# Padding tiles that move three groups of matmul operands to other offsets within a 512-byte line

## The chip, the cores and the metric

The kernel runs on one core of one Trainium2 chip. The metric is the device time of one execution in microseconds (us); the time given for a kernel is the median of its runs.

## The reference

Two layers of a decoder trunk on 512 tokens of width 1024, everything in float32. Each layer is a half-step feed-forward block, a mixer, and a second half-step feed-forward block:

```
def swiglu(h, w_up, w_down):
    gate, up = jnp.split(h @ w_up, 2, axis=-1)
    return (jax.nn.silu(gate) * up) @ w_down
...
for l in range(DEPTH):
    x = x + 0.5 * swiglu(rms_norm(x, ffn1_norm[l]), ffn1_w_up[l], ffn1_w_down[l])
    h = rms_norm(x, mix_norm[l])
    proj = h @ w_in[l]
    q, k, v, z, xbc, dt_raw, gate_sb, gate_ssm = jnp.split(proj, IN_SPLITS, axis=-1)
    ... y_sb = stick_breaking_attention(q, k, v) @ w_branch_sb[l]      # 4 heads x 128
    ... y_ssm = mamba2_mixer(z, xbc, dt_raw, ...) @ w_branch_ssm[l]    # 24 heads x 64, 8 groups
    merged = sigmoid(gate_sb) * y_sb + sigmoid(gate_ssm) * y_ssm
    x = x + merged @ w_out[l]
    x = x + 0.5 * swiglu(rms_norm(x, ffn2_norm[l]), ffn2_w_up[l], ffn2_w_down[l])
return rms_norm(x, final_norm)
```

The hidden width of the feed-forward block is 2816, that is 22 blocks of 128.

## The kernel before

**Layout.** All activations are kept transposed: a tile has 128 channels in its 128 partitions and the 512 tokens along the free axis (2048 bytes of a partition). A weight unit is 128 x 1024 floats: eight blocks of 128 x 128, one per block of input channels.

**Products in three parts.** TensorE works on rounded float32 (`fp32r`). To keep full precision each operand is split into a rounded part and a rest: weights into `whi` and `wlo` (`convert`, L282 on ScalarE and L284 on VectorE), normalised inputs into `hhi` and `hlo`, hidden activations into two `act` tiles, and so on. `mm3` (L315 to L317) then issues three matmuls for each 128 x 128 block: high weights by high input, low weights by high input, high weights by low input. Each of the three loads a stationary operand of 128 x 128 (a load of weights, which runs beside the matmul before it) and streams a moving operand of 256 or 512 columns. In most units the weights are stationary and the activations move; in `by_tokens` (v and z) it is the other way round.

**The feed-forward block** (`ffn`) runs three slices of 8, 8 and 6 hidden blocks. Most hidden blocks are computed in pairs by `pair_of_blocks`, which gets two blocks' gate and up products for both halves of the tokens from seven half-width products (`SEVEN`) on sums of weights and on differences of inputs. The differences are made once per block by `combine`: their rounded parts are the tiles `th`, their rests the tiles `tl`, and the products on them have 256 columns. Four of the seven products (s2, s1, s3 and 22) move `th` and `tl`; the other three (11, 12 and s4) move halves of `hhi` and `hlo`. The activated results are split into `act` tiles, and the `down` units multiply these, 512 columns at a time, into the output.

**The mixer** (`mixer`) makes q, k and v (tiles `yt`), runs the attention, whose outputs are the tiles `ohi` and `olo` of pool `yo`, then the convolution and the state-space scan, whose outputs are again `yt` tiles. The branch products `bsb` (moving `ohi`, `olo`) and `bssm` (moving `yt`) and the output projection `out` (moving `mhi`, `mlo`) follow.

**Order.** The whole program is in an order written by hand: each engine executes its instructions in the order of issue. Side work (activations, splits, conversions of the next weight units) is held in generators, and `tick` advances them by a step after each group of matmuls, so that VectorE, ScalarE and GpSimd work beside TensorE. Weights are fetched by the SP queue four units ahead and converted two units ahead.

**Where tiles lie.** Tile pools are stacked: those of the left side grow from low addresses of a partition, those with `side="right"` grow downwards from the top. Nearly all tiles are multiples of 512 bytes long, so that a pool gives its offset within a 512-byte line to all of its tiles and to the pools stacked on it. In the program before, these offsets are:

| tiles | side | offset in a 512-byte line | less the weights' offset |
|---|---|---|---|
| `whi`, `wlo` (weights), `wraw` | left | 96 | 0 |
| `hhi`, `hlo` | left | 96 | 0 |
| `act`, and stacked on it `s1`, `s2`, `s3`, `g`, `a`, `c` | left | 96 | 0 |
| `mhi`, `mlo`, most tiles of the mixer's pool | left | 96 | 0 |
| `x`, and `uv`, `th`, `tl` stacked on it | right | 480 | 384 |
| `yo` (`ohi`, `olo`), `yt`, under a tile `edge` of 384 bytes | right | 96 | 0 |

The tile `edge` is allocated and never written or read.

Of the kernel before, what the change touches and what calls it, by code (L numbers as in the profile page):

```python
# [17 lines left out]
P = 128  # L18
# [95 lines left out]
def pairs_from(layer, f):  # L114

    return 6 if (layer, f) == (0, 1) else 2


def unit_order(layer):

    def ffn(f):
        for s, (j0, j1) in enumerate(SLICES):
# [7 lines left out]
            for m in OUT_ORDER:  # L130
                yield (layer, f, "down", s, m), j1 - j0

    yield from ffn(1)
    for t, h in qkv_order():
        yield (layer, t, h), KB
# [13 lines left out]
    for m in OUT_ORDER:  # L149
        yield (layer, "out", m), KB  # L150
    yield from ffn(2)


# [10 lines left out]
class Builder:  # L164
# [581 lines left out]
    def ffn(self, layer, f, gain, gain_next):  # L746
        tc = self.tc
        with tc.tile_pool(name=f"act{layer}{f}", bufs=8, reuse_waits="tile") as ap, \
                tc.tile_pool(name=f"sx{layer}{f}", bufs=2, reuse_waits="tile") as self.sx, \
                tc.tile_pool(name=f"ffn{layer}{f}", bufs=3, reuse_waits="tile") as fp:  # L750
            self.gated = {}
            for s, (j0, j1) in enumerate(SLICES):
                act = []
                last = s == len(SLICES) - 1
                for j in range(j0, j1):
                    if j % 2 == 0:
                        two = self.pair(ap, ("act", "act"), (P, 2 * SEQ))
                        act += [tuple(t[:, i * SEQ:(i + 1) * SEQ] for t in two) for i in range(2)]
                    if j >= pairs_from(layer, f):
                        if j % 2 == 0:  # L760
                            self.pair_of_blocks((layer, f, "pair", j), fp, two)
                        continue
                    g = self.t(fp, [P, SEQ], "g", bufs=4)
                    if self.pos == 0:
                        pg, pu = self.opening(gain)
                        self.spawn(self.gate(pg, g))
                        for k in range(KB // 2):
                            self.spawn(self.combine(k, gain), 12 + 14 * k)
                    else:
                        pg = self.product(self.h, layer, f, "gate", j)  # L770
                        self.spawn(self.gate(pg, g))
                        pu = self.product(self.h, layer, f, "up", j)
                    self.spawn(self.up(pu, g, fp, act[-2 + j % 2]))
                n, both = j1 - j0, []
                for m in OUT_ORDER[:2]:
                    both.append((self.t(self.pmm, [P, SEQ], "mm"), self.unit(layer, f, "down", s, m, ahead=m == 0)))
                    self.dense(*both[-1], act, 0, n - 2, stop=False)
                for i, m in enumerate(OUT_ORDER):
                    if last and gain_next is None and i == KB - 3:
                        self.ending((layer, f, "down", s), act, n, fp)  # L780
                        break
                    if i < 2:
                        if i:
                            self.ahead(1)
                        ps = both[i][0]
                        self.dense(*both[i], act, n - 2, n, start=False, base=0)
                    else:
                        ps = self.t(self.pmm, [P, SEQ], "mm")
                        self.dense(ps, self.unit(layer, f, "down", s, m), act, 0, n)
                    if last and i == 0:  # L790
                        self.norm_start()
                        self.xd = self.t(self.dr, [KB, P, SEQ], "xd") if f == 1 else None
                        if f == 1:
                            self.close_t()
                    self.spawn(self.down(ps, m, gain_next, last))
# [476 lines left out]
    def mixer(self, layer):  # L1272
# [13 lines left out]
        with ExitStack() as mix:  # L1286
            enter = mix.enter_context
            branches = ExitStack()
            edge = branches.enter_context(
                tc.tile_pool(name=f"edge{layer}", bufs=1, side="right", reuse_waits="tile"))  # L1290
            self.t(edge, [P, 96], "edge")
            self.yo = branches.enter_context(
                tc.tile_pool(name=f"yo{layer}", bufs=SBH, side="right", reuse_waits="tile"))
            self.yt = branches.enter_context(
# [88 lines left out]

    def open_t(self):

        self.tpool = self.tc.tile_pool(name=self.name("tpool"), bufs=2, side="right", reuse_waits="tile")
        self.tp = self.tpool.__enter__()

    def close_t(self):
        self.tpool.__exit__(None, None, None)  # L1390
        self.tp = None

    def build(self):
# [141 lines left out]
```

## Time and profile before

| | |
|---|---|
| median of 3 runs | 2582.1 us (2581.85 to 2583.41) |
| the profiled execution | 2582.94 us, its span from the first to the last instruction 2581.2 us |
| TensorE matmuls (PE) | 15028, busy 2559.8 us of the span |
| TensorE loads of weights (PEld) | 15028, busy 2288.4 us |
| VectorE (DVE) / ScalarE (ACT) / GpSimd (POOL) | busy 1752.4 / 1282.0 / 498.5 us |
| granted TensorE clock | 0.999 of full speed |

In the trace the rows of successive matmuls overlap, and the ends of matmuls are modelled. A row's duration is therefore longer than the time that a product costs in a dense stretch; that time is the distance from one start to the next, which is called the pitch here.

### The profile page before, as it was taken

What the parts mean: (1) busy time and instruction counts of PE and PEld (TensorE: products, weight loads), DVE (VectorE), ACT (ScalarE), POOL (GpSimd) and SP (SyncE); (2) the same over time, 40 slices, a digit from 0 to 9 for tenths busy, and PEclk for the clock granted to TensorE, in tenths of its full rate; (3) what the DMA queues carried; (4) which work ended last, traced back from release to release, by engine and by line L of the source; (5) the groups of instructions that cost most, each with busy time, mean ns of one, the idle gap of its engine ahead of it and who ended that gap; (6) DMA issues with size and microseconds to landing.
All of it is one profiled execution on the core that took longest, in us unless ns stands there. A gap on an engine that the chain in (4) does not pass through costs nothing.

```text
span 2581.2 us, 38169 instructions
## 1 busy us (share of the span) xinstructions
PE 2559.8 (99%) x15028; PEld 2288.4 (89%) x15028; DVE 1752.4 (68%) x2426; ACT 1282.0 (50%) x2103; POOL 498.5 (19%) x614
## 2 busy tenths in 40 slices
PE   9999999999999999999999999999999999999998
PEld 7898988888888889899998989888888888899997
DVE  8575875676664478586885858756676644876766
ACT  6343556665554255343653535566555533543444
POOL 0121201143341002121121312012333310022120
PEclk9999999999999999999999999999999999999999
DMA  6454542233333454545364545423333334455452
GB/s 183 138 159 136 132 138 87 99 103 110 101 105 107 139 162 139 164 139 164 106 180 139 156 141 136 139 72 111 99 103 104 116 109 143 152 143 168 142 162 78
DMA packets 104659, 335.76 MB, mean 130 GB/s; under 512 B 11872, under 2 KB 15392, under 8 KB 104480
## 3 DMA queue, kind: packets, MB, share of 16 engines
q1 hardware_dynamic: 92672, 292.84, 34.2%
q0 software_dynamic: 10944, 39.85, 8.6%
q8 instruction: 118, 1.93, 0.3%
q10 hardware_dynamic: 864, 0.64, 0.1%
q14 instruction: 61, 0.50, 0.1%
HBM read 320.60 MB, written 12.68 MB: 129 GB/s over the span
## 4 chain that ended last, share of the span: by engine, by line
PE 93%; DVE 4%; ACT 2%; issue 1%; DMA 0%; POOL 0%; SPq 0%; DVEq 0%; ACTq 0%
PE mm L315 26%; PE mm L317 25%; PE mm L316 25%; PE pa L316 3%; PE pa L317 3%; PE pa L315 3%; PE pa L1169 2%; DVE wlo L284 1%; PE pa L1171 1%; PE pt L853 1%; PE pt L1154 1%; DVE cv L1027 1%; PE pt L1152 1%; ACT whi L282 1%; PE pa L453 0%
## 5 line engine op out<-in xcount | busy, mean ns | idle before, releaser
L282 ACT CAST whi<-wraw 128x1024 fp32r<-128x1024 f32 (+3 forms) x440 | 435.1, 989 | 584.9 <-PE mm L317 485.0
L284 DVE TENSOR_TENSOR wlo<-wraw,whi 128x1024 fp32r<-128x1024 f32 (+3 forms) x440 | 538.7, 1224 | 165.9 <-ACT whi L282 164.5
L315 PE MATMUL mm<-hhi,whi 128*128 128x512 f32 (+1 forms) x1584 | 565.1, 357 | 0.0
L317 PE MATMUL mm<-hlo,whi 128*128 128x512 f32 (+1 forms) x1584 | 554.1, 350 | 0.4 <-DVE hlo L507 0.4
L316 PE MATMUL mm<-hhi,wlo 128*128 128x512 f32 (+1 forms) x1584 | 553.0, 349 | 0.0
L317 PEld LDWEIGHTS mm<-hlo,whi 128*128 128x128 f32 x1584 | 299.9, 189 | 40.3 <-DVE hlo L507 0.8
L316 PEld LDWEIGHTS mm<-hhi,wlo 128*128 128x128 f32 x1584 | 300.4, 190 | 34.6 <-DVE wlo L284 0.2
L315 PEld LDWEIGHTS mm<-hhi,whi 128*128 128x128 f32 x1584 | 300.3, 190 | 34.2 <-ACT hhi L505 0.4
L284 DVE TENSOR_TENSOR wlo<-s,whi 128x1024 fp32r<-128x1024 f32 x152 | 235.2, 1561 | 60.4 <-ACT whi L282 60.4
L315 PE MATMUL mm<-act,whi 128*128 128x512 f32 (+1 forms) x710 | 274.2, 386 | 0.0
L317 PE MATMUL mm<-act,whi 128*128 128x512 f32 (+1 forms) x710 | 274.2, 386 | 0.0
L316 PE MATMUL mm<-act,wlo 128*128 128x512 f32 (+1 forms) x710 | 274.1, 386 | 0.0
L315 PE MATMUL mm<-th,whi 128*128 128x256 f32 x912 | 257.4, 282 | 0.0
L317 PE MATMUL mm<-tl,whi 128*128 128x256 f32 x912 | 257.0, 282 | 0.0
L316 PE MATMUL mm<-th,wlo 128*128 128x256 f32 x912 | 256.9, 282 | 0.0
L626 POOL TENSOR_TENSOR g<-g,rs 128x512 f32<-128x512 f32 x76 | 132.5, 1744 | 553.4 <-DVE g L633 534.3
L282 ACT CAST whi<-s 128x1024 fp32r<-128x1024 f32 x152 | 159.3, 1048 | 102.4 <-PE mm L317 60.7
L652 DVE SCALAR_TENSOR_TENSOR x<-mm,x 128x512 f32<-128x512 f32 x93 | 64.1, 689 | 196.0 <-PE mm L317 196.0
L254 POOL DMA_DIRECT2D s<-in_wflat_dram x76 | 65.6, 863 | 621.3 <-DMA s<-in_wflat_dram 332.4
L315 PEld LDWEIGHTS mm<-th,whi 128*128 128x128 f32 x912 | 172.4, 189 | 0.0
L316 PEld LDWEIGHTS mm<-th,wlo 128*128 128x128 f32 x912 | 172.0, 189 | 0.0
L317 PEld LDWEIGHTS mm<-tl,whi 128*128 128x128 f32 x912 | 171.9, 188 | 0.0
(306 smaller groups left out, 5088.9 us busy)
## 6 DMA issues: line engine op xcount, KB each, us to landing
wraw<-in_wflat_dram SPq DMA_DIRECT2D x328, 512.0 KB, 3.6
s<-in_wflat_dram SPq DMA_DIRECT2D x76, 512.0 KB, 4.7
s<-in_wflat_dram POOLq DMA_DIRECT2D x76, 512.0 KB, 7.4
wraw<-in_wflat_dram SPq DMA_DIRECT2D x88, 384.0 KB, 3.1
cumb<-cum_d SPq DMA_DIRECT2D x16, 768.0 KB, 4.8
xd<-x SPq DMA_DIRECT2D x16, 256.0 KB, 3.2
wraw<-in_wflat_dram SPq DMA_DIRECT2D x16, 256.0 KB, 3.6
x<-xd SPq DMA_DIRECT2D x16, 256.0 KB, 3.9
```

The costliest lines, as they stand in the source:

```text
L254: self.nc.gpsimd.dma_start(raw, src, accum_op=ALU.add)
L282: nc.scalar.copy(hi[:, :n], raw[:, :n])
L284: nc.vector.tensor_tensor(lo[:, :n], raw[:, :n], hi[:, :n].bitcast(F32), op=ALU.subtract)
L315: mm(ps, a[0], b[0], start=start, stop=False, **kw)
L316: mm(ps, a[1], b[0], start=False, stop=False, **kw)
L317: mm(ps, a[0], b[1], start=False, stop=stop, **kw)
L626: eng.tensor_tensor(r, r, self.rs[:, cols].unsqueeze(1).to_broadcast([P, 2, half]), op=ALU.mult)
L652: self.nc.vector.scalar_tensor_tensor(x, pd, 0.5, x, op0=ALU.mult, op1=ALU.add)
L853: self.nc.tensor.transpose(pt[:, cs], src[:, cs], self.ident)
L1027: nc.vector.scalar_tensor_tensor(u[:, j:], ps[:, :SEQ - j], tap[KCONV - 1 - j], u[:, j:], op0=ALU.mult, op1=ALU.add)
L1152: nc.tensor.matmul(pc[:, :P], bt[:, span(c)], ct[:, span(c)], start=True, stop=True)
L1169: nc.tensor.matmul(py[:, i * HD:(i + 1) * HD], decs[c][:, i, :], xdts[c][:, i, :], start=True, stop=True)
```

## The change

Three tiles that nothing writes or reads move the tiles stacked behind them:

- A tile `gap` of 192 bytes is the first of pool `act`. The `act` tiles, and the pools `sx` (`s1`, `s2`, `s3`) and `ffn` (`g`, `a`, `c`) stacked on them, move up by 192 bytes: offset 288, 192 off the weights'.
- A tile `rim` of 320 bytes in a pool of its own is opened just before the pool of `uv`, `th` and `tl`, and closed just after it. These move down by 320 bytes: from offset 480 to 160, 64 off the weights'. The `x` tiles stay.
- The tile `edge` shrinks from 384 to 352 bytes. The tiles of `yo` and `yt` move up by 32 bytes: offset 128, 32 off the weights'.

No instruction, order or transfer is written differently.

```
@@ ffn
             self.gated = {}
+            self.t(ap, [P, 48], "gap", bufs=1)
             for s, (j0, j1) in enumerate(SLICES):
@@ mixer
-            self.t(edge, [P, 96], "edge")
+            self.t(edge, [P, 88], "edge")
@@ open_t
+        self.rim = self.tc.tile_pool(name=self.name("rim"), bufs=1, side="right", reuse_waits="tile")
+        self.t(self.rim.__enter__(), [P, 80], "rim")
         self.tpool = self.tc.tile_pool(name=self.name("tpool"), bufs=2, side="right", reuse_waits="tile")
@@ close_t
         self.tpool.__exit__(None, None, None)
+        self.rim.__exit__(None, None, None)
         self.tp = None
```

`reuse_waits="tile"` means that a new tile waits for the last uses of those older tiles whose bytes it overlaps.

More of the change, by code (lines that the diff above doesn't have):

```diff
@@ L751, in ffn @@
             self.gated = {}
+            self.t(ap, [P, 48], "gap", bufs=1)
             for s, (j0, j1) in enumerate(SLICES):
@@ L1290, in mixer @@
                 tc.tile_pool(name=f"edge{layer}", bufs=1, side="right", reuse_waits="tile"))
-            self.t(edge, [P, 96], "edge")
+            self.t(edge, [P, 88], "edge")
             self.yo = branches.enter_context(
@@ L1384, in open_t @@
     def open_t(self):
+        self.rim = self.tc.tile_pool(name=self.name("rim"), bufs=1, side="right", reuse_waits="tile")
+        self.t(self.rim.__enter__(), [P, 80], "rim")
         self.tpool = self.tc.tile_pool(name=self.name("tpool"), bufs=2, side="right", reuse_waits="tile")
@@ L1390, in close_t @@
         self.tpool.__exit__(None, None, None)
+        self.rim.__exit__(None, None, None)
         self.tp = None
```

## The prediction

> **What bounds the kernel now.** I read the page's busy times first, then its chain of work that ended last.
>
> ```profile
> span 2581.2 us, 38169 instructions
> PE 2559.8 (99%) x15028; PEld 2288.4 (89%) x15028; DVE 1752.4 (68%) x2426; ACT 1282.0 (50%) x2103; POOL 498.5 (19%) x614
> ...
> PE 93%; DVE 4%; ACT 2%; issue 1%; DMA 0%; POOL 0%; SPq 0%; DVEq 0%; ACTq 0%
> PE mm L315 26%; PE mm L317 25%; PE mm L316 25%; PE pa L316 3%; PE pa L317 3%; PE pa L315 3%; PE pa L1169 2%; DVE wlo L284 1%; PE pa L1171 1%; PE pt L853 1%; PE pt L1154 1%; DVE cv L1027 1%; PE pt L1152 1%; ACT whi L282 1%; PE pa L453 0%
> ```
>
> TensorE is on 93% of the chain, and the three matmuls of `mm3` (L315 to L317) alone on 85%. The change adds no instruction, so the only price at stake is the pitch of these products: nanoseconds from one start to the next, times a count. Next the groups of instructions, with shapes kept apart, for the counts. I show the L315 rows; L316 and L317 have as many each, so a group's products are three times its row.
>
> ```profile
> L315 PE MATMUL mm<-hhi,whi 128*128 128x512 f32 x976 | 392.9, 403 | 0.0
> L315 PE MATMUL mm<-act,whi 128*128 128x512 f32 x686 | 267.2, 389 | 0.0
> L315 PE MATMUL mm<-th,whi 128*128 128x256 f32 x912 | 257.4, 282 | 0.0
> L315 PE MATMUL mm<-hhi,whi 128*128 128x256 f32 x608 | 172.1, 283 | 0.0
> L315 PE MATMUL pa<-th,whi 128*128 128x256 f32 x304 | 85.5, 281 | 0.0
> L315 PE MATMUL mm<-yt,whi 128*128 128x512 f32 x192 | 74.8, 390 | 0.0
> L315 PE MATMUL mm<-ohi,whi 128*128 128x512 f32 x64 | 25.3, 396 | 0.0
> L315 PE MATMUL mm<-act,whi 128*128 128x256 f32 x24 | 7.0, 291 | 0.0
> L315 PE MATMUL pa<-act,whi 128*128 128x256 f32 x12 | 3.4, 283 | 0.0
> ```
>
> What the change moves: on `th` and `tl`, 3 x (912 + 304) = 3648 products of 256 columns; on `act`, 3 x 686 = 2058 of 512 columns and 3 x 36 = 108 of 256; on `yt` and `ohi`/`olo`, 3 x (192 + 64) = 768 of 512 columns. Together 2826 of 512 and 3756 of 256. It leaves `hhi`/`hlo` (among them 3 x 976 and 3 x 608 here) at offset 0. The durations (282 and 283, 389 and 390) say nothing on the offset, as their ends are modelled. So I went to the starts, in order of time, at the borders of pure stretches.
>
> ```profile
> 92.85 0.40 PE L315 MATMUL mm<-act,whi 128*128 128x512 f32 x1
> 93.09 0.40 PE L316 MATMUL mm<-act,wlo 128*128 128x512 f32 x1
> 93.32 0.40 PE L317 MATMUL mm<-act,whi 128*128 128x512 f32 x1
> 93.56 0.39 PE L315 MATMUL mm<-act,whi 128*128 128x512 f32 x1
> 93.78 0.39 PE L316 MATMUL mm<-act,wlo 128*128 128x512 f32 x1
> ...
> 94.94 0.39 PE L315 MATMUL mm<-act,whi 128*128 128x512 f32 x1
> ...
> 136.42 0.28 PE L315 MATMUL mm<-hhi,whi 128*128 128x256 f32 x1
> ...
> 142.17 0.28 PE L315 MATMUL mm<-th,whi 128*128 128x256 f32 x1
> ...
> 150.72 0.28 PE L315 MATMUL pa<-hhi,whi 128*128 128x256 f32 x1
> ...
> 470.72 0.33 PE L968 MATMUL pa<-short,ntri 128*128 128x128 f32 x2
> 470.89 0.45 PE L315 MATMUL mm<-hhi,whi 128*128 128x512 f32 x1
> ...
> 885.80 0.39 PE L315 MATMUL mm<-yt,whi 128*128 128x512 f32 x1
> ...
> 902.12 0.39 PE L315 MATMUL mm<-mhi,whi 128*128 128x512 f32 x1
> ```
>
> The counts between these starts come from the busy times by stretch (the number after PE's busy time also holds one or two matmuls whose rows reach in from before: 2, 1, 2 and 1 in the first four).
>
> ```profile
> 92.84:136.41 43.57, 43.57 (x194) 36.07 (x193) 18.86 (x21) 9.58 (x10) 1.73 (x2) 1.00 0.55 168
> 136.41:142.16 5.75, 5.75 (x49) 5.74 (x48) 3.02 (x3) 2.58 (x3) 0.00 (x0) 1.00 0.11 46
> 142.16:150.71 8.55, 8.55 (x74) 8.55 (x73) 6.75 (x6) 4.63 (x6) 5.10 (x4) 1.00 0.63 152
> 885.79:902.11 16.32, 16.32 (x73) 13.52 (x72) 8.00 (x10) 4.41 (x5) 0.00 (x0) 1.00 0.48 148
> 140.00:214.00 74.00, 74.00 (x623) 74.00 (x622) 63.92 (x59) 40.15 (x52) 23.97 (x18) 1.00 0.56 150
> ```
>
> The columns are the stretch, its length, then busy time and count of PE, of the weight loads, DVE, ACT and POOL, the granted clock, the DMA share and GB/s. So:
>
> - `act`, 512 columns, offset 0: 43.57 us / 192 = 226.9 ns. `yt`, offset 0: 16.32 / 72 = 226.7 ns.
> - `hhi`, 256 columns, offset 0: 5.75 / 48 = 119.8 ns.
> - `th`, 256 columns, offset 384: 8.55 / 72 = 118.75 ns.
>
> From 256 to 512 columns at offset 0 the pitch grows by 226.7 - 119.8 = 106.9 ns, so a product costs 106.9 ns for each 256 columns and a fixed 12.9 ns. The fixed part is what an offset can touch. Two readings say that it does. At offset 384 it is 118.75 - 106.9 = 11.85 ns, 1.05 less than at offset 0, in products alike in all but the tiles. And within one stretch at one offset it isn't steady at first: the starts from 92.85 to 94.94 are 0.24, 0.23, 0.24 and 0.22 us apart and nine of them take 2.09 us, 232 ns each, before the stretch falls to 226.7. So the cost depends on how the two reading streams, the moving operand and the next weights, meet, and that has several outcomes.
>
> **The change part by part.** The sum is made against the profiled execution, 2582.94 us (its span is 2581.2), 0.8 above the median of 2582.1.
>
> `rim` (`th`, `tl`): from 384 to 64 off the weights, 3648 products. Upper bound of a gain: two 128-column products from 470.72 to 470.89 take 0.17 us where they stream 2 x 53 ns (half of 106.9 each); the first had its weights loaded beside the matmul before, so the second waited for its own, about 0.17 - 0.06 = 0.11 us. A 256-column product cannot go below its weight load, so 118.75 can fall to some 112: at most 6.7 x 3648 = 24.6 us. On the other side the nearest row is offset 0, 119.8: +1.05 x 3648 = +3.8 us; twice that rise would be +7.7.
>
> `gap` and `edge` (`act`, `yt`, `ohi`, `olo`): from 0 to 192 and 32 off the weights, 2826 products of 512 columns. Upper bound of a gain: all of the fixed 12.9 ns, 36.5 us. On the other side: the 232 ns of the first nine `act` products for good, +5.2 x 2826 = +14.7 us.
>
> Between these ends I take the value near the one offset that the trace compares, which gave 1.05 ns of 12.9, but not at it: that one is an arbitrary offset, and the stretch above swings by 10 ns between neighbours. I take twice it, 2.1 to 2.2 ns, for all three groups: 2.2 x 6582 = 14.5 us. The 108 `act` products of 256 columns are in that count.
>
> The rest has one answer, nothing. The padding issues nothing. VectorE, ScalarE and GpSimd read and write the moved tiles in the same lengths; beside the products in the feed-forward pairs DVE is busy 63.92 of 74.00 us, and that is the cover of a faster TensorE: it would give out only where the pitch falls by more than 14%, and the bound above for `th` is 6%. The stretch with `act` has DVE at 18.86 of 43.57. The new borders let an `act` tile of 4096 bytes reach 192 bytes into one more older tile; the tiles concerned (gates, merged inputs) are read by products that stand ahead on TensorE of those whose results fill `act`, so the wait is over when it is asked for. `th` and `tl` overlap the same two older tiles each, by other amounts. What is queued behind such a wait on ACT (the split's cast) and DVE (its rest) would be the next weight conversions, which are two units ahead, and those units take 24 x 0.119 = 2.9 us each at the least.
>
> Sum: 2582.9 - 14.5 = 2568.4, against the median 2567.6. I predict 2568 us.
>
> A rule stands against the whole change. The Trainium skill (TensorE: Matmul & The Clock Gate, step-by-step part of "What happens when you issue a matmul") says that TensorE has two independent SBUF read ports, one for the moving operand and one for the loads of weights, so that "Loading the next tile's weights doesn't steal SBUF read bandwidth from the running matmul"; SBUF — State Buffer, "Who interferes with whom", adds that "PE and ACT never wait on anyone". By that the offset is worth nothing and the time stays 2582. The pitches of 119.8 and 118.75 do not agree with it for products alike in form, but by 1 ns only; the fixed 12.9 ns may still be something that no offset moves.
>
> **The rivals.**
>
> Nothing changes (0.25). The fixed cost belongs to changing the weights, and the 1.05 ns is a peculiarity of 256 columns, where the load of about 112 ns fills nearly the whole pitch. For it: `act` and `yt` settle on the same 226.7 to 226.9. Against it: the slow start of each `act` stretch. Then only `th` and `tl` move, by -1 to +1 ns: 2582 - 4 to 2582 + 4, that is 2578 to 2586, centre 2582. It is also the case in which the padding doesn't do what it says. The skill's rule above comes to this result.
>
> Most of the fixed cost goes (0.15). At the new offsets the two streams never meet: 12.9 x 2826 + 6.7 x 3648 = 61 us, 2521; I count from a gain of 30 us, 2552, on.
>
> Slower (0.20). One mechanism: at offset 0 the 512-column products settle into an even pitch after nine of them, and at 192 and 32 they never settle. The place is the `down`, `bsb` and `bssm` units, the price 5.2 ns on 2826 products, +14.7 us: 2597. With `th` back at the cost of offset 0 it would be 2601. It decides from 5.2 us / 2826 = 1.8 ns per product on. For it: at 512 columns the even pitch is seen only at offset 0, and the trace has no other offset there. Against it: with 256 columns the mean at 384 is lower, not higher.
>
> **How the numbers follow.** My forecast, a gain of 6 to 30 us (2552 to 2576), has 0.40, the large gain 0.15, no change 0.25, slower 0.20. A measurement of this kernel can tell about 0.2%, 5.2 us. Faster by over 0.2%: 0.40 + 0.15 = 0.55; within: 0.25; slower: 0.20. The time is that of the likeliest case, 2568. For the range I leave out the lower half of the large gain (below 2537, 0.08 to 0.09) and the slower case beyond its own price (above 2598, 0.1): 2537 to 2598. The forecast's own range is 2552 to 2576.
>
> **What would show it.** In the changed kernel's rows of starts, stretches of 72 `th` products should take 116.5 ns each (8.39 us instead of 8.55), the 192 `act` products 224.7 ns (43.1 us instead of 43.57), the 72 `yt` products 224.5 (16.16 us instead of 16.32), while 48 `hhi` products stay at 5.75 us. If `act` and `yt` stay at 226.7 the offset has no hold on 512 columns; if `act` stays near 232 the slower rival has come. If the pitches fall and the span does not, DVE has taken over in the pairs: its idle time there would be gone. What would make the prediction most wrong is that the fixed cost is a threshold thing, all or nothing at an offset: then the gain is several times mine, or the loss is.

## The result: slower by 0.6%, all of it in the products of 512 columns

| | before | after |
|---|---|---|
| median | 2582.2 us | 2597.3 us |
| ratio, 95% interval | | 1.0058 (1.0047 to 1.0070) |
| span of the profiled execution | 2581.2 us | 2595.6 us |

The forecast was 2568 us. The time landed 15.1 us above the kernel before, at the price that the prediction had given its rival "slower" (2597 us).

The page of the changed kernel, first its busy times:

```profile
span 2595.6 us, 38169 instructions
PE 2575.1 (99%) x15028; PEld 2285.6 (88%) x15028; DVE 1754.6 (68%) x2426; ACT 1281.7 (49%) x2103; POOL 500.1 (19%) x614
```

The counts of instructions are the same on each engine; PE is busy 15.3 us longer, no other engine differs by more than 3 us, and the part of the span in which PE is not busy goes from 21.4 to 20.5 us. So there is no new wait: the products themselves take longer. The stretches that answer to those shown before (length, busy time and count of PE, loads of weights, DVE, ACT, POOL, granted clock, DMA share, GB/s):

```profile
137.03:142.78 5.75, 5.75 (x49) 5.73 (x48) 3.02 (x3) 2.59 (x3) 0.00 (x0) 1.00 0.11 43
142.78:151.27 8.49, 8.49 (x74) 8.49 (x73) 6.75 (x6) 4.64 (x6) 5.14 (x4) 1.00 0.59 150
216.86:261.65 44.79, 44.79 (x194) 36.11 (x193) 18.88 (x21) 9.56 (x10) 1.74 (x2) 1.00 0.55 164
890.19:906.99 16.80, 16.80 (x73) 13.50 (x72) 7.93 (x10) 4.40 (x5) 0.00 (x0) 1.00 0.47 141
```

They hold 48 `hhi`, 72 `th`/`tl`, 192 `act` and 72 `yt` products (and one or two rows that reach in). The pitch is 5.75 / 48 = 119.8 ns for `hhi` as before, 8.49 / 72 = 117.9 for `th` (118.75 before), 44.79 / 192 = 233.3 for `act` (226.9) and 16.80 / 72 = 233.3 for `yt` (226.7). With the pitch of one stretch taken for all products of its kind, and that of `yt` for `ohi` and `olo` too:

| moved | pitch | products | us |
|---|---|---|---|
| `th`, `tl` | -0.9 ns | 3648 | -3.3 |
| `act`, 512 columns | +6.4 ns | 2058 | +13.2 |
| `yt`, `ohi`, `olo` | +6.6 ns | 768 | +5.1 |
| sum | | | +15.0 |

That is nearly the whole of the 15.1 us between the medians; the two profiled spans lie 14.4 us apart. The starts show that the slow `act` stretch is not unsteady:

```profile
216.87 0.39 PE L315 MATMUL mm<-act,whi 128*128 128x512 f32 x1
217.09 0.40 PE L316 MATMUL mm<-act,wlo 128*128 128x512 f32 x1
217.33 0.40 PE L317 MATMUL mm<-act,whi 128*128 128x512 f32 x1
...
218.26 0.40 PE L315 MATMUL mm<-act,whi 128*128 128x512 f32 x1
...
261.66 0.28 PE L315 MATMUL mm<-hhi,whi 128*128 128x256 f32 x1
```

The second product starts at 217.09 and the seventh at 218.26: five pitches of 0.234 us, the same as in the whole stretch. It has settled at once, in another and dearer cycle. The groups of instructions show the same:

```profile
L315 PE MATMUL mm<-act,whi 128*128 128x512 f32 x686 | 271.2, 395 | 0.0
...
L315 PE MATMUL mm<-th,whi 128*128 128x256 f32 x912 | 255.6, 280 | 0.0
```

389 became 395 ns and 282 became 280. The prediction set these means aside because the ends are modelled; in fact they went the way of the pitch, though they are no exact measure of it: 6 ns against 6.4 for `act`, 2 against 0.9 for `th`.

### The profile page after: what moved, and what is told of

Read it like the earlier page. It is cut to its first block, busy times and chain, and to the rows that moved or that the text cites. A ratio compares the mean times of both kernels' runs of the same rounds, so it can differ in the third digit from the quotient of the medians.

```text
span 2595.6 us, 38169 instructions
## 1 busy us (share of the span) xinstructions
PE 2575.1 (99%) x15028; PEld 2285.6 (88%) x15028; DVE 1754.6 (68%) x2426; ACT 1281.7 (49%) x2103; POOL 500.1 (19%) x614
## 4 chain that ended last, share of the span: by engine, by line
PE 92%; DVE 5%; ACT 2%; issue 1%; DMA 1%; POOL 0%; SPq 0%; DVEq 0%; ACTq 0%
PE mm L315 26%; PE mm L317 26%; PE mm L316 25%; PE pa L315 3%; PE pa L317 3%; PE pa L316 3%; PE pa L1170 2%; DVE wlo L284 1%; PE pa L1172 1%; PE pt L854 1%; PE pt L1155 1%; ACT whi L282 1%; DVE cv L1028 1%; PE pt L1153 1%; PE pa L854 0%
## 5 line engine op out<-in xcount | busy, mean ns | idle before, releaser
L315 PE MATMUL mm<-hhi,whi 128*128 128x512 f32 (+1 forms) x1584 | 564.5, 356 | 0.0
L317 PE MATMUL mm<-hlo,whi 128*128 128x512 f32 (+1 forms) x1584 | 553.7, 350 | 0.0
L316 PE MATMUL mm<-hhi,wlo 128*128 128x512 f32 (+1 forms) x1584 | 552.4, 349 | 0.1
L317 PEld LDWEIGHTS mm<-hlo,whi 128*128 128x128 f32 x1584 | 299.6, 189 | 39.8 <-DVE hlo L507 0.2
L316 PEld LDWEIGHTS mm<-hhi,wlo 128*128 128x128 f32 x1584 | 300.1, 189 | 35.1 <-DVE wlo L284 0.6
L315 PEld LDWEIGHTS mm<-hhi,whi 128*128 128x128 f32 x1584 | 300.1, 189 | 34.2
L315 PE MATMUL mm<-act,whi 128*128 128x512 f32 (+1 forms) x710 | 278.1, 392 | 0.0
L316 PE MATMUL mm<-act,wlo 128*128 128x512 f32 (+1 forms) x710 | 278.1, 392 | 0.0
L317 PE MATMUL mm<-act,whi 128*128 128x512 f32 (+1 forms) x710 | 278.1, 392 | 0.0
L315 PE MATMUL mm<-th,whi 128*128 128x256 f32 x912 | 255.6, 280 | 0.0
L316 PE MATMUL mm<-th,wlo 128*128 128x256 f32 x912 | 254.4, 279 | 0.0
L317 PE MATMUL mm<-tl,whi 128*128 128x256 f32 x912 | 254.4, 279 | 0.0
L315 PEld LDWEIGHTS mm<-th,whi 128*128 128x128 f32 x912 | 171.5, 188 | 0.0
L317 PEld LDWEIGHTS mm<-tl,whi 128*128 128x128 f32 x912 | 171.4, 188 | 0.0
L316 PEld LDWEIGHTS mm<-th,wlo 128*128 128x128 f32 x912 | 171.0, 187 | 0.0
```

What stands on the lines that cost most here:

```text
L315: mm(ps, a[0], b[0], start=start, stop=False, **kw)
L316: mm(ps, a[1], b[0], start=False, stop=False, **kw)
L317: mm(ps, a[0], b[1], start=False, stop=stop, **kw)
```

## The experiments

Theory 1: TensorE pays a fixed cost per product that is set by the distance between moving operand and weights within a line of bytes, and by the number of columns; nothing else in the change counts. Rival 2: what counts is where a tile lies, not its distance to the weights. Rival 3: `act` products are slow because other engines read and write the tiles that were moved with `act`.

### The rim alone

The kernel before with `rim` (320 bytes), no `gap`, `edge` at 384 bytes.

```
+        self.rim = self.tc.tile_pool(name=self.name("rim"), bufs=1, side="right", reuse_waits="tile")
+        self.t(self.rim.__enter__(), [P, 80], "rim")
...
+        self.rim.__exit__(None, None, None)
```

> Only the tile rim is kept: th and tl at 64 off the weights, act, yt and yo back at 0. Theory 1 (the offset between the moving operand and the weights within a 512-byte line sets a fixed cost per product, and nothing else counts): the 3648 th and tl products take 117.8 ns instead of 118.7 as in the changed kernel, act and yt are back at 226.7 to 226.9 ns, and the time is 2582.2 - 3.3 + at most 0.8 for the hhi products behind them, 2579 to 2580 us. Rival 2 (what counts is where a tile lies, not its distance to the weights): the same here, this run does not tell them apart. Rival 3 (the slower act products come from other engines that write and read the moved g, a, c and s tiles): the same here too.

2579.6 us, ratio 0.9992 (0.9982 to 1.0001): -2.5 us. The groups of instructions:

```profile
L315 PE MATMUL mm<-act,whi 128*128 128x512 f32 x686 | 267.2, 389 | 0.0
...
L315 PE MATMUL mm<-th,whi 128*128 128x256 f32 x912 | 255.5, 280 | 0.0
```

`act` is back at 389 and `th` keeps its 280. The interval holds 1, so the time alone does not show a gain. The pitches do: `th` alone would give -3.3 us, and in the whole trace the 2736 `hhi` products of 256 columns, which did not move, start 120.0 ns apart where it was 119.7 before, which takes some 0.9 us back.

### The gap alone

```
+            self.t(ap, [P, 48], "gap", bufs=1)
```

> Only the tile gap is kept: act and the tiles stacked on it 192 bytes up, th, tl, yt, yo as before. Theory 1: the 2058 act products of 512 columns take 233.3 ns instead of 226.9, +13.1 us, and the time is 2595 us; yt stays at 226.7. Rival 2: the same. Rival 3: the same. With the first run it says whether the parts add up: the edge's part would then be 768 x 6.5 = 5.0 us, and 2582.2 - 2.5 + 13.1 + 5.0 = 2597.8 against 2597.3 measured for all three.

2594.3 us, ratio 1.0047 (1.0032 to 1.0062): +12.1 us. Busy times by stretch, 192 `act` and 72 `yt` products:

```profile
216.62:261.42 44.80, 44.80 (x194) 36.11 (x193) 18.87 (x21) 9.57 (x10) 1.74 (x2) 1.00 0.55 163
888.14:904.46 16.32, 16.32 (x73) 13.52 (x72) 8.01 (x10) 4.40 (x5) 0.00 (x0) 1.00 0.45 144
```

`act` at 233.3, `yt` at 226.7. With the rim's -2.5 this leaves 15.1 - 12.1 + 2.5 = 5.5 us for the edge, which was not run alone, against 5.1 worked out. So the parts add up as far as was run.

### The neighbours of act moved, act itself not

```
+                tc.tile_pool(name=f"gap2{layer}{f}", bufs=1, reuse_waits="tile") as g2, \
                 tc.tile_pool(name=f"sx{layer}{f}", bufs=2, reuse_waits="tile") as self.sx, \
...
+            self.t(g2, [P, 48], "gap2")
```

> The 192 bytes are put behind act instead of ahead of it: act stays 0 off the weights, and only s1, s2, s3, g, a and c, which TensorE never reads, lie at 288. Theory 1: act at 226.9 ns, time unchanged within 0.1%, 2582 us. Rival 3: act at 233.3 ns and 2595 us as with the whole gap.

2582.1 us, ratio 0.9999 (0.9990 to 1.0008).

```profile
215.69:259.26 43.57, 43.57 (x194) 36.06 (x193) 18.88 (x21) 9.58 (x10) 1.74 (x2) 1.00 0.55 165
```

43.57 / 192 = 226.9 ns. Rival 3 falls: `s1` to `c` at their new places cost nothing that can be seen.

### The weights moved, with act beside them

```
+        self.t(enter(tc.tile_pool(name="wpad", bufs=1)), [P, 48], "wpad")
         self.wraw = enter(tc.tile_pool(name="wraw", bufs=3))
```

> A tile of 192 bytes is put between the pool of hhi and hlo and the weights' pools, and none of the three paddings of the change is there (edge is at its 384 bytes). Weights, act, mhi and mlo all lie at 288 in the line: act and mhi are 0 off the weights as before, though act lies just where it lay in the changed kernel; hhi, yt and yo stay where they were and are now 320 off the weights, th and tl 192. Theory 1: act and mhi stay at 226.7 to 226.9 ns; hhi and yt with 512 columns leave 226.7, probably for the 233.3 of the two offsets seen (+6.6 x (3072 + 768) = +25 us), so the time rises to about 2600 to 2610 us, depending on the 256-column products (1 ns on 6384 of them is 6 us). Rival 2: act goes to 233.3 ns (+13 us), hhi and yt stay, 2595 us.

2575.4 us, ratio 0.9973 (0.9963 to 0.9983), faster where I expected slower. Stretches of 192 `hhi` products of 512 columns, twice 48 `hhi` of 256 columns with 72 `th` behind them, 192 `act` and 72 `yt`:

```profile
28.91:72.85 43.94, 43.94 (x193) 36.06 (x192) 37.23 (x58) 25.28 (x37) 1.89 (x2) 1.00 0.51 144
72.85:78.51 5.66, 5.66 (x49) 5.64 (x48) 3.57 (x4) 3.10 (x4) 0.00 (x0) 1.00 0.01 3
78.51:86.68 8.17, 8.17 (x74) 8.17 (x73) 6.66 (x6) 4.64 (x6) 3.50 (x2) 1.00 0.24 64
...
155.55:161.21 5.66, 5.66 (x50) 5.66 (x49) 5.57 (x8) 3.63 (x5) 0.00 (x0) 1.00 0.55 187
161.21:169.68 8.47, 8.47 (x74) 8.47 (x73) 7.11 (x6) 4.64 (x6) 5.23 (x4) 1.00 0.61 151
214.91:258.43 43.52, 43.52 (x194) 36.05 (x193) 18.92 (x21) 9.58 (x10) 1.74 (x2) 1.00 0.55 167
885.74:902.22 16.48, 16.48 (x73) 13.52 (x72) 7.98 (x10) 4.41 (x5) 0.00 (x0) 1.00 0.45 146
```

`act` lies at 288 in the line, exactly where it cost 233.3 ns, and takes 43.52 / 192 = 226.7. `hhi` and `yt`, which did not move, go to 228.9 ns, both alike. `th`, now at 192, runs at 8.47 / 72 = 117.6 in the stretch from 161.21 us and in most others, at 8.17 / 72 = 113.5 in the one from 78.51 us and some others. Ahead of both stand 48 `hhi` products at the same distance of 320 and the same pitch, 5.66 / 48 = 117.9. Rival 2 falls: the distance counts. What I had wrong is the price at 320: 228.9, not 233.3, while the 256-column products got cheaper.

### A sweep of offsets

Four runs, each with padding before the weights (`wpad`), before `act` (`gap`), before `yo` and `yt` (`edge`) and before `th` and `tl` (`rim`), so that each gives five distances.

| run | wpad | gap | edge | rim | time, one execution |
|---|---|---|---|---|---|
| a | 64 | 64 | 192 | 288 | 2581.0 us |
| b | 128 | 256 | 160 | 0 | 2600.7 us |
| c | 256 | 160 | 160 | 32 | 2606.2 us |
| d | 480 | 352 | 0 | 288 | 2604.3 us |

The edit of run a, with four bytes to each column; the others differ in the sizes, and a size of 0 has no tile:

```
+            self.t(ap, [P, 16], "gap", bufs=1)
...
-            self.t(edge, [P, 96], "edge")
+            self.t(edge, [P, 48], "edge")
...
+        self.t(self.rim.__enter__(), [P, 72], "rim")
...
+        self.t(enter(tc.tile_pool(name="wpad", bufs=1)), [P, 16], "wpad")
```

> A sweep of offsets: a tile of 64 bytes between hhi/hlo and the weights, gap 64, edge 192, rim 288 bytes. Off the weights now lie hhi and hlo 448, act 64, yt and yo 128, th and tl 32; mhi stays at 0. Theory 1a (offset 0 is the only cheap one for 512 columns): hhi, act and yt each between 229 and 233.3 ns, mhi at 226.7; with 5898 such products at +2 to +6.6 ns that is +12 to +39 us less some 6 to 10 us at the 256-column products, 2585 to 2612 us. Theory 1b (the cost changes from offset to offset by no such rule, and 0 isn't the lowest): some of the three below 226.7.

> 128 bytes ahead of the weights, gap 256, edge 160, rim 0. Off the weights: hhi and hlo 384, act 256, yt and yo 96, th and tl 256. Theory 1 in itself: hhi with 256 columns takes 118.7 ns, as th did at 384 in the kernel before, against 119.85 at 0. If the kind of tile counts and not the offset, it stays at 119.85. Theory 1a: hhi, act, yt at 229 to 233.3 ns for 512 columns, 2585 to 2612 us; theory 1b: some below 226.7.

> 256 bytes ahead of the weights, gap 160, edge 160, rim 32. Off the weights: hhi and hlo 256, act 160, yt and yo 480, th and tl 96. Theory 1: hhi with 256 columns as th at 256 in the run with 128 bytes ahead of the weights, to 0.3 ns. Theory 1a: hhi, act and yt at 229 to 233.3 ns for 512 columns, 2585 to 2612 us; theory 1b: some below 226.7.

> 480 bytes ahead of the weights, gap 352, no edge, rim 288. Off the weights: hhi and hlo 32, act 352, yt and yo 416, th and tl 128. Theory 1: hhi with 512 columns at 233.3 ns, as yt at 32 in the changed kernel (+20 us on 3072), and hhi with 256 columns as th at 32 in the run with 64 bytes ahead of the weights; act near the 228.9 of hhi and yt at 320. Time about 2600 us. If the kind of tile counts, hhi stays at 226.7 in its settled stretches.

The stretches that the table below is worked out from are told apart by the count behind PE: x193 holds 192 `hhi` products of 512 columns, x194 holds 192 `act`, x73 behind 880 us holds 72 `yt`, x74 holds 72 `th`, x50 and x49 hold 48 `hhi` of 256 columns. Run a:

```profile
29.04:73.83 44.79, 44.79 (x193) 36.10 (x192) 37.26 (x57) 25.17 (x37) 1.89 (x2) 1.00 0.50 139
137.39:143.04 5.65, 5.65 (x49) 5.64 (x48) 2.97 (x3) 2.58 (x3) 0.00 (x0) 1.00 0.12 49
162.44:170.84 8.40, 8.40 (x74) 8.40 (x73) 7.49 (x6) 4.74 (x6) 5.27 (x4) 1.00 0.55 142
215.18:259.14 43.96, 43.96 (x194) 36.07 (x193) 19.04 (x21) 9.55 (x10) 1.74 (x2) 1.00 0.55 167
156.98:162.44 5.46, 5.46 (x50) 5.46 (x49) 5.37 (x8) 3.63 (x5) 0.00 (x0) 1.00 0.58 200
889.87:906.67 16.80, 16.80 (x73) 13.52 (x72) 7.93 (x10) 4.38 (x5) 0.00 (x0) 1.00 0.46 144
```

Run b:

```profile
28.64:73.26 44.62, 44.62 (x193) 36.17 (x192) 37.31 (x57) 25.18 (x37) 1.88 (x2) 1.00 0.51 140
157.00:162.69 5.69, 5.69 (x50) 5.69 (x49) 5.61 (x8) 3.71 (x5) 0.00 (x0) 1.00 0.59 186
162.69:171.32 8.63, 8.63 (x74) 8.63 (x73) 6.95 (x6) 4.63 (x6) 5.14 (x4) 1.00 0.59 159
217.17:260.72 43.55, 43.55 (x194) 36.05 (x193) 18.83 (x21) 9.58 (x10) 1.74 (x2) 1.00 0.55 166
```

Run c:

```profile
28.40:71.94 43.54, 43.54 (x193) 36.04 (x192) 37.19 (x57) 25.40 (x37) 1.88 (x2) 1.00 0.52 145
157.21:162.97 5.76, 5.76 (x50) 5.76 (x49) 5.67 (x8) 3.72 (x5) 0.00 (x0) 1.00 0.56 184
162.97:171.61 8.64, 8.64 (x74) 8.64 (x73) 6.88 (x6) 4.64 (x6) 5.13 (x4) 1.00 0.59 152
217.65:262.63 44.98, 44.98 (x194) 36.18 (x193) 18.83 (x21) 9.56 (x10) 1.74 (x2) 1.00 0.54 164
891.94:908.74 16.80, 16.80 (x73) 13.52 (x72) 7.93 (x10) 4.40 (x5) 0.00 (x0) 1.00 0.45 148
```

Run d:

```profile
28.75:73.54 44.79, 44.79 (x193) 35.98 (x192) 37.09 (x57) 25.16 (x37) 1.89 (x2) 1.00 0.51 138
157.96:163.57 5.61, 5.61 (x50) 5.61 (x49) 5.52 (x8) 3.63 (x5) 0.00 (x0) 1.00 0.58 192
163.57:172.11 8.54, 8.54 (x74) 8.54 (x73) 7.17 (x6) 4.64 (x6) 5.22 (x4) 1.00 0.57 152
217.34:262.14 44.80, 44.80 (x194) 36.05 (x193) 18.92 (x21) 9.56 (x10) 1.74 (x2) 1.00 0.55 163
895.10:911.96 16.86, 16.86 (x73) 13.56 (x72) 7.90 (x10) 4.39 (x5) 0.00 (x0) 1.00 0.46 149
```

Length over count, by the distance to the weights modulo 256 bytes (the larger distance it was measured at behind the tile's name):

| modulo 256 | 512 columns, ns | 256 columns, ns |
|---|---|---|
| 0 | 226.9 `act`, 226.7 `yt` before; 226.8 `act` 256, `hhi` 256 | 119.8 `hhi` before; 119.9 `th` 256, 120.0 `hhi` 256 |
| 32 | 233.3 `yt` after, `hhi` | 116.7 `th`; 116.9 `hhi` |
| 64 | 228.9 `hhi` 320, `yt` 320; 229.0 `act` | 117.9 `th` after, `hhi` 320 |
| 96 | 233.3 `act` 352 | 120.0 `th` |
| 128 | 233.3 `yt`; 232.4 `hhi` 384 | 118.75 `th` 384 before; 118.6 `th`; 118.5 `hhi` 384 |
| 160 | 234.3 `act`; 234.2 `yt` 416 | no long stretch |
| 192 | 233.3 `act` after, `hhi` 448 | 113.75 and 117.7 `hhi` 448; 113.5 and 117.6 `th` in the run with the weights moved |
| 224 | 233.3 `yt` 480 | no long stretch |

Wherever this table has a distance on two kinds of tile they agree within 1 ns, except at 192, where `hhi` and `th` each have two values 4 ns apart. Not all expectations held: run a came out below its range of 2585 to 2612 us, and in run d `act` at 352 took 233.3 ns, not the 228.9 seen at 320. Theory 1 stands, with three corrections. The period is 256 bytes, not 512. Theory 1a holds only in that 0 modulo 256 is the lowest for 512 columns; for 256 columns 0 is nearly the dearest. And the cost is not one fixed sum per product: 192 is dear at 512 columns and has the cheapest value at 256. So run c, with `hhi` at 256, has its `hhi` at 226.8 and still is the slowest: `act` at 160 and `yt` at 224 have the dear offsets, and `th` at 96 takes 120.0 ns.

### The low weights moved alone

```
+            hi = self.t(self.wsp, [P, KB * P], "whi", F32R)
+            if not w:
+                self.t(self.wsp, [P, 8], "wmid", bufs=1)
+            lo = self.t(self.wsp, [P, KB * P], "wlo", F32R)
+            if not w:
+                self.t(self.wsp, [P, 56], "wend", bufs=1)
...
-            self.t(edge, [P, 96], "edge")
+            self.t(edge, [P, 32], "edge")
```

> Only the low weights wlo are moved, by 32 bytes, with 224 bytes behind them so that act and the rest stay a multiple of 256 off whi; edge is 128 for the same reason. So each moving operand of 512 columns is 0 or 256 off whi, and 480 or 224 off wlo. Theory 1 says that the reads of the moving operand meet those of the weights that are loaded beside it, which are the next product's: then the product at L315 (beside it wlo is loaded) takes 233.3 ns and those at L316 and L317 (beside them whi is loaded) 226.7, 228.9 in the mean of three. If a product meets its own weights instead, the slow one is L316, which uses wlo. In both cases the 512-column products cost +2.2 ns in the mean, 6402 x 2.2 = 14 us, and the time is about 2596 us, less or more what th and tl do.

2606.3 us in one execution, 10 us above the expected 2596. The `yt` rows of the three lines, all at 389 to 390 ns before:

```profile
L315 PE MATMUL mm<-yt,whi 128*128 128x512 f32 x192 | 76.8, 400 | 0.0
...
L317 PE MATMUL mm<-yt,whi 128*128 128x512 f32 x192 | 75.9, 395 | 0.0
...
L316 PE MATMUL mm<-yt,wlo 128*128 128x512 f32 x192 | 74.8, 389 | 0.0
```

The slowest product is the one beside which `wlo` is loaded (L315), and the one that uses `wlo` (L316) is as fast as before: the order that was expected if a product meets the weights loaded beside it. But the product at L317, with nothing moved beside it, costs 6 ns too, and the three together are as dear as if all had a wrong distance, 16.80 / 72 = 233.3 ns each:

```profile
894.53:911.33 16.80, 16.80 (x73) 13.52 (x72) 7.93 (x10) 4.40 (x5) 0.00 (x0) 1.00 0.47 144
```

Nor does the order decide. In the run with the weights moved, where `yt` lies 320 off `whi` and `wlo` alike, the three lines stand in the same order:

```profile
L315 PE MATMUL mm<-yt,whi 128*128 128x512 f32 x192 | 75.6, 394 | 0.0
L317 PE MATMUL mm<-yt,whi 128*128 128x512 f32 x192 | 75.3, 392 | 0.0
L316 PE MATMUL mm<-yt,wlo 128*128 128x512 f32 x192 | 74.5, 388 | 0.0
```

So moving `wlo` alone off the distance of 0 is enough to make these products dear. Whether a product meets its own weights or the next one's, and how that reaches the products behind it, stays open.

### The rim at 192, and the lowest offsets together

The kernel before with a rim of 192 bytes alone, the edit of the first experiment with another size:

```
+        self.t(self.rim.__enter__(), [P, 48], "rim")
```

> Only a rim of 192 bytes: th and tl 192 off the weights, all others at 0 as before. In the run with the weights moved, th and tl at 192 ran at 113.4 ns in some stretches and at 117.7 in others. Theory 1 with memory (which of the two cycles is entered depends on the products just before): behind hhi products at 119.85 ns one of the two in every stretch; 117.7 gives 2582.2 - 1.0 x 3648 = 2578.5 us, 113.4 gives 2582.2 - 5.3 x 3648 = 2563 us. A rival in which chance decides in each stretch gives a mixture.

2562.7 us, ratio 0.9924 (0.9909 to 0.9938): faster than both kernels, by 19.5 us against before. One stretch of 72 `th` products, and a longer one through the pairs of blocks:

```profile
159.99:168.17 8.18, 8.18 (x74) 8.18 (x73) 7.03 (x6) 4.64 (x6) 5.26 (x4) 1.00 0.52 149
...
140.00:212.00 72.00, 72.00 (x623) 72.00 (x622) 64.88 (x61) 39.85 (x51) 24.45 (x18) 1.00 0.59 156
```

8.18 / 72 = 113.6 ns, 5.15 below before: x 3648 = 18.8 us, nearly all of the gain. That is close to the bound of about 112 that the prediction drew from the weight loads. DVE is now busy 64.88 of 72.00 us beside them, 90%, and still covers: PE is busy in all 72.00 us.

The second kernel has `wpad` 192, `edge` 192, `rim` 160:

```
-            self.t(edge, [P, 96], "edge")
+            self.t(edge, [P, 48], "edge")
...
+        self.t(self.rim.__enter__(), [P, 40], "rim")
...
+        self.t(enter(tc.tile_pool(name="wpad", bufs=1)), [P, 48], "wpad")
```

> The lowest costs of the sweep together: 192 bytes ahead of the weights, edge 192, rim 160. act, mhi, yt and yo 0 off the weights, hhi and hlo 320, th and tl 32. Theory 1: act, yt and mhi at 226.7 ns, th and tl at 116.7 (-7.5 us), hhi with 512 columns at 228.9 (+4 to +7 us), hhi with 256 columns at 117.85 (-5.5 us) or, if products at 32 ahead of them lead into the faster cycle, at 113.4 (-17.5 us): 2573 or 2561 us. If the costs do not add up it is not below the 2575.4 of the run with the weights moved.

2572.6 us, ratio 0.9961 (0.9946 to 0.9976): the smaller of the two gains, and the first of the two times expected. Its `hhi` rows, 512 and 256 columns:

```profile
L315 PE MATMUL mm<-hhi,whi 128*128 128x512 f32 x976 | 394.1, 404 | 0.0
...
L315 PE MATMUL mm<-hhi,whi 128*128 128x256 f32 x608 | 170.0, 280 | 0.0
```

At 64 modulo 256 the 256-column `hhi` products gained a little (rows of 280 ns against 283 before) and not what the faster cycle would have given; those of 512 columns cost more (404 against 403).

### Period, or the products ahead?

A rim of 96 bytes alone (`th` at 288), 24 columns in the line of the first experiment:

```
+        self.t(self.rim.__enter__(), [P, 24], "rim")
```

> The smallest change: only a rim of 96 bytes, th and tl 288 off the weights (32 beyond a multiple of 256), all others at 0 as before. Theory 1 with a period of 256 bytes: th and tl at 116.7 ns as at 32, -2.05 x 3648 = -7.5 us, 2574.7 us, act, yt and hhi unchanged. If the period were 512 bytes, 288 would be an offset of its own with another cost.

A rim of 352 alone, 88 columns (`th` at 32), and one of 448, 112 columns (`th` at 448, that is 192 modulo 256):

> Only a rim of 352 bytes: th and tl 32 off the weights, all others at 0. If the period is 256 bytes and the products ahead pick the cycle, 117.9 ns as at 288 and 2579 us; if 32 and 288 differ, 116.7 ns and 2574.7 us.

> Only a rim of 448 bytes: th and tl 448 off the weights, all others at 0. If the period is 256 bytes, 113.6 ns as at 192 and 2563 us; if the line is 512 bytes, some other value, by the offsets seen between 116.7 and 120 ns, 2575 to 2587 us.

2579.1 us at 288 (ratio 0.9987, 0.9978 to 0.9997), 2579.0 at 32, 2563.2 at 448, the last two from one execution each. The group of `th` products at 288:

```profile
L315 PE MATMUL mm<-th,whi 128*128 128x256 f32 x912 | 256.0, 281 | 0.0
```

The same group at 32:

```profile
L315 PE MATMUL mm<-th,whi 128*128 128x256 f32 x912 | 255.7, 280 | 0.0
```

And at 448:

```profile
L315 PE MATMUL mm<-th,whi 128*128 128x256 f32 x912 | 252.5, 277 | 0.0
```

At 192, in the run with the rim of 192 bytes:

```profile
L315 PE MATMUL mm<-th,whi 128*128 128x256 f32 x912 | 252.9, 277 | 0.0
```

288 acts as 32 and 448 as 192: the period of 256 bytes holds. But at 288 the time is 4.4 us above the 2574.7 expected, for the same distance gives `th` 116.7 ns behind `hhi` at 448 in run a and about 117.9 here behind `hhi` at 0 (2582.2 - 2579.0 = 3.2 us over 3648), as 192 gives 113.6 behind `hhi` at 0 and 117.6 behind `hhi` at 320. That the distance of the products ahead picks between such cycles is not shown: with the weights moved, `th` ran at 113.5 and at 117.6 ns behind `hhi` at 320 in one and the same run. What picks the cycle was not found.

## Why the prediction was wrong, point by point

- **What bounds the kernel, and the counts: right.** Pitch times count gives 15.0 of the 15.1 us.
- **The term for `act`, `yt`, `ohi` and `olo`: wrong in sign.** It took -2.2 ns on 2826 products, -6.2 us; they cost +6.4 and +6.6 ns, +18.3 us. The step that failed is the choice of a value near "the one offset that the trace compares". That row compares 256-column products at 384 with 256-column products at 0; it was carried to 512 columns, where the order is the other way round: there 0 modulo 256 is the cheapest of all eight offsets run, and any move from it costs 2 to 8 ns. Behind it stands the split into 106.9 ns for each 256 columns and a fixed 12.9 ns that an offset can touch, for both widths alike. The split holds at the one offset that it was drawn from: at 192 the two widths differ by 233.3 - 113.6 = 119.7 ns, more than the whole 256-column product costs, so no fixed part is left.
- **The term for `th` and `tl`: right in sign, too large.** -2.2 ns was taken, -0.9 came. The value at 64 is one of a scattered set (113.6 to 120.0), not a step of common size.
- **That one other offset can stand for the rest: the assumption behind both.** The prediction named what would break it, a fixed cost that is a matter of all or nothing at an offset, but gave it no chance of its own.
- **The slower rival: right in place, near in price, wrong in mechanism.** Place: the 512-column products; price 5.2 ns against 6.4 to 6.6. But they do settle, into a cycle of 233.3 ns. That its 2597 us was met to 0.3 us is luck: it had the 512-column products 3.6 us too cheap and left out the 3.3 us that `th` and `tl` gave back.
- **The rival that nothing changes fell.** The Trainium skill (TensorE: Matmul & The Clock Gate, "What happens when you issue a matmul") says that loading the next weights takes no read bandwidth from the running matmul. Here the pitch of 512-column products goes from 226.7 to 234.3 ns with the distance between the two operands alone. The measurement decides against what the prediction drew from the rule, that the offset is worth nothing; that it is the two reads that meet was not shown.
- **DVE as cover, the new overlaps of tiles, the moved reads of other engines: right.** They cost nothing that can be seen (0.9999 with the neighbours moved, and no more time without a busy PE than before).

The upper bound of a gain was well drawn for `th`: 6.7 ns were allowed, 5.15 were there to be had, at 192 and not at 64. For 512 columns all of 12.9 ns was allowed, and none of the seven other offsets run gave anything. One reading of rows behind the bound was off without harm: by the starts in the trace the wait of 0.11 us for a load lies ahead of the product that follows the two of 128 columns, not between these two.

## What to carry to other kernels

Where TensorE is the bound, the pitch of dense stretches is worth reading per operand and width: here the address distance between the streamed operand and the weights, modulo 256 bytes, was worth between -0.8% and +0.9% of the whole kernel without a single instruction changed. A value read at one width or one distance says nothing on another, so sweep the distance for each width apart (one kernel can carry several), take the cheapest (here 0 for 512 columns and 192 for 256), and measure the combination too: with 256 columns a distance can have two prices.

## What the runs showed of the hardware that was not expected

- The pitch of a settled stretch of 512-column products takes few values: 226.7 ns at 0 modulo 256, 228.9 at 64, and 232.4 to 234.3 at the others.
- At 256 columns the order is another: 119.8 at 0, 120.0 at 96, 113.6 or 117.6 at 192.
- At one distance a stretch of 256-column products can run in two steady cycles (113.6 and 117.6 ns at 192). What picks one was not found: in the run with the weights moved both occurred in one layout, behind the same products.
